# The low parts of the projections' split weights: a negation on ScalarE and an accumulating DMA in place of a subtraction on VectorE

## The chip, the cores and the metric

The kernel runs on one core of one Trainium2 chip. The metric is device time in microseconds (us), lower is better: the median of 3 runs. A profile of one further execution, taken by the hardware profiler, tells what each engine did when.

## The reference, cut to what matters

One layer of a decoder with 1088 token columns (1024 prompt positions and 64 sample tokens) and a width of 1024, all in float32:

```python
p = rmsnorm(x, norm1) @ w_in                  # 1024 -> 1536: 512 for S5, 1024 for the chunked gMLP
o_s5 = S5 scan of p[:, :512], then gelu, then g * sigmoid(g @ w_glu + b_glu)
o_cm = u * (tril(W_s) v + b)                  # 8 heads, chunks of 128 positions
x = x + concat(rmsnorm(o_s5), rmsnorm(o_cm)) @ w_out
x = x + (silu(h @ w_gate) * (h @ w_up)) @ w_down   # h = rmsnorm(x), 22 tiles of 128 hidden columns
y = rmsnorm(x)
```

The projections' weights that the change is about are w_in (12 chunks), w_out (14 chunk loads) and w_glu (2 chunks). A chunk is 128 partitions by 1024 float32 values, 512 KB, and each partition's 4 KB lie together in DRAM.

## The kernel before, in words

TensorE multiplies in a rounded format (float32r). So every operand is split into a high part (the value rounded) and a low part (the value minus its high part), and each product is three matmuls: high by high, high by low, low by high (`mm3`, lines 143 to 146). L144, L145 and L146 in the profile are these three. For `pu`, `po` and `pg` the weight's low part is read by L146; for `pv`, where the weights are the moving operand, by L145.

A split is made by `split` (lines 139 to 141): ScalarE copies the raw chunk into the high tile (L140), VectorE subtracts the high tile from the raw chunk into the low tile (L141). `load_q` (L224) takes a raw buffer (three of 4 KB per partition turn about), has SyncE load the chunk (L227) and splits it. Its high and low tiles are three slots each in one buffer, `cwr` in the profile; later w_out chunks use the same slots (`WO`) and a fourth one in `fb`. A slot is written anew only when TensorE has done its last matmul with the chunk that was there. In a quarter of w_in, chunk 0 holds the first four k-tiles and chunk 1 the last four. For quarters 1 to 5, so, the slot for one chunk of the next quarter comes free shortly before that quarter begins.

The work goes in this order. Quarters 0 and 1 of w_in make the S5 input (`s5_in`), while VectorE computes the S5 tables and the norms of three groups of columns. At the start GpSimd computes `dt` and `mag`, each with a power instruction (L212). Quarters 2 and 3 make v (`v_quarter`), quarters 4 and 5 make u (`cm_out`), with the eight steps of the S5 scan (`s5_a`, `s5_b`, `s5_c`) between them. Then come the GLU with w_glu (`glu`), the output projection (`wo_tile`, `wo_last`) and, from about 428 us to the end, the feed-forward part, a seven-product scheme whose weights are split by a function of its own (`wsplit`), which the change leaves alone.

Each engine takes its instructions from a queue in order. The order on each queue is planned when the kernel is built, from the framework's own estimate of durations (`schedule_with_timeline_sim=True`), with the order of the program text as priority; a few `issue_after` lines pin single places. Here GpSimd issues no DMA before the change: all loads and stores go out on SyncE's queue.

Of the kernel before, what the change touches and what calls it, by code (L numbers as in the profile page):

```python
# [10 lines left out]
F32 = mybir.dt.float32  # L11
F32R = mybir.dt.float32r
I32 = mybir.dt.int32
AF = mybir.ActivationFunctionType
ALU = mybir.AluOpType
# [67 lines left out]
def layer_kernel(ctx: ExitStack, tc: tile.TileContext, A, O, dbg=None):  # L83
    nc = tc.nc
    V, S, P, PE, Q = nc.vector, nc.scalar, nc.gpsimd, nc.tensor, nc.sync
# [46 lines left out]
    def raw(name, shape):  # L132
        n = int(np.prod(shape))
        t = rawp.tile([128, 1024], F32, tag="raw", name=name, bufs=3)[:, :n]
        if len(shape) == 2:
            t = t.rearrange("p (a b) -> p a b", a=shape[0])
        return t

    def split(src, hi, lo, eng=None):
        S.activation(hi, src, AF.Copy)  # L140
        return (eng or V).tensor_tensor(lo, src, hi.bitcast(F32), ALU.subtract)  # L141

    def mm3(p, wh, wl, ah, al, start, stop):
        PE.matmul(p, wh, ah, start=start, stop=False)  # L144
        PE.matmul(p, wh, al, start=False, stop=False)  # L145
        return PE.matmul(p, wl, ah, start=False, stop=stop)  # L146
# [77 lines left out]
    def load_q(key, src, to=None):  # L224

        r = raw(f"w{key[0]}{key[1]}{key[2]}", (4, 256))
        Q.dma_start(r, src)  # L227
        h, l = to or [wqp.tile([128, 4, 256], F32R, tag=x, name=x) for x in ("wqh", "wql")]
        split(r, h, l)
        WQ[key] = (h, l)  # L230

    def load_wq(q):
        for half in range(2):
            load_q(("i", q, half), A["w_in"][q, :, 4 * half:4 * half + 4, :])
# [33 lines left out]
    def fm_group(q, c, tag="mm"):  # L268

        n0, n = CH[c]  # L270
        pp = [bank(f"pu{m}", tag)[:, :n] for m in range(2)]
        km = [(k, m) for k in range(8) for m in range(2)]
        for k, m in km if q == 0 else sorted(km, key=lambda x: x[1]):
            wh, wl = wq(q, k, slice(128 * m, 128 * m + 128))
            MM[q, c] = mm3(pp[m], wh, wl, xh[:, k, n0:n0 + n], xl[:, k, n0:n0 + n], k == 0, k == 7)
        return pp
# [13 lines left out]

    load_x(0, 0)
    load_q(("i", 0, 0), A["w_in"][0, :, 0:4, :])
    load_x(0, 1)
    load_q(("i", 0, 1), A["w_in"][0, :, 4:8, :])
    load_x(0, 2)
    load_x(0, 3)
# [298 lines left out]
    r = raw("bdr", (8, 64))  # L595
# [16 lines left out]
    r = raw("wsr", (8, 128))  # L612
# [4 lines left out]
    for q in range(2):  # L617
# [3 lines left out]
        for i in range(4):  # L621
            m, h = divmod(4 * q + i, 2)
# [6 lines left out]
    def v_quarter(q, j):  # L629
        p = bank("pv")  # L630
        for k in range(8):
            wh, wl = wq(q, k, slice(0, 256))
            mm3(p[:, 0:256], xh[:, k, tok(j)], xl[:, k, tok(j)], wh, wl, k == 0, k == 7)
        S.activation(v[:, j, 256 * (q - 2):256 * (q - 1)], p[:, 0:256], AF.Gelu_apprx_tanh, scale=r1c[:, j:j + 1])
# [98 lines left out]
    wgh = gl.tile([128, 4, W], F32R, name="wgh")  # L733
    wgl = gl.tile([128, 4, W], F32R, name="wgl")
    for i in range(2):
        r = raw(f"wg{i}", (2, W))
        Q.dma_start(r, A["w_glu"][:, 2 * i:2 * i + 2, :])
        split(r, wgh[:, 2 * i:2 * i + 2, :], wgl[:, 2 * i:2 * i + 2, :])
    G5 = []
    for m in range(4):  # L740
        g5 = gl.tile([128, 8, 136], F32, name=f"g5{m}")
# [9 lines left out]
    def glu(c):  # L751
        n0, n = CH[c]
        acc = ACC5[c] = gl.tile([128, 384], F32, tag="acc", name="acc", bufs=3)[:, :n]
        for m in range(4):
            p = bank("pg", "s5" if m % 2 else "mm")
            for k in range(4):
                mm3(p[:, :n], wgh[:, k, 128 * m:128 * m + 128], wgl[:, k, 128 * m:128 * m + 128],
                    xh[:, k, n0:n0 + n], xl[:, k, n0:n0 + n], k == 0, k == 3)
            sg = gl.tile([128, 384], F32, tag="sg", name="sg", bufs=2)[:, :n]
            S.activation(sg, p[:, :n], AF.Sigmoid, bias=gcol("bglu", m))  # L760
            z = tc2n(G5[m], n0, n)
            V.tensor_tensor(z, z, nat(sg), ALU.mult)
            accum_sq(gl, nat(acc), z, m == 0)
# [27 lines left out]
    i = 0  # L791
# [519 lines left out]
```

## Time and profile before

| | |
|---|---|
| median of 3 runs | 1127.18 us (1125.74 to 1130.81) |
| the profiled execution's own time | 1127.69 us |
| its span, first to last instruction | 1125.6 us |
| TensorE's mean granted clock in it | 0.982 |
| TensorE busy | 1056.9 us, 94% |
| VectorE busy | 907.8 us, 81% |
| ScalarE busy | 449.4 us, 40% |
| GpSimd busy | 316.3 us, 28% |

The rows below name engines as PE (TensorE matmul), PEld (TensorE weight load), DVE (VectorE), ACT (ScalarE), POOL (GpSimd) and SP (SyncE). L140 is line 140 of the kernel. A tile pair `cwr<-wi` reads "writes cwr from wi". Busy shares are averages over the span; the stretches of the kernel have different limits.

### The profile page before, as it was taken

To read this page: it belongs to the slowest core of one execution; us is meant where nothing else is said; L and a number is where in the kernel's file an instruction comes from. 1 tells how busy PE (TensorE), PEld (TensorE's weight loads), DVE (VectorE), ACT (ScalarE), POOL (GpSimd) and SP (SyncE) were. 2 spreads that over 40 slices of the span, in tenths; PEclk is the share of its full clock that TensorE was granted. 3 is DMA by queue.
4 is the path that set the end of the run, shared out by engine and by line. 5 is a ranking of instruction groups with operands and counts; after the bars stand their busy time and mean duration, and the time that the engine had idled before them with its cause. 6 is when DMAs were issued, how large, how long until landed. Compare 5 with 4: busy or idle time off the path is not lost.

```text
span 1125.6 us, 20406 instructions
## 1 busy us (share of the span) xinstructions
PE 1056.9 (94%) x7966; PEld 1029.3 (91%) x7966; DVE 907.8 (81%) x1780; ACT 449.4 (40%) x822; POOL 316.3 (28%) x287
## 2 busy tenths in 40 slices
PE   7799999978899989999999999999999999999994
PEld 6789999868799879999999999999998899899994
DVE  6987999889999897667657656657668979879998
ACT  7314334398454442232232232233234324425561
POOL 5010330000000344334334334435434331223220
PEclk9989999989899899999999999999999999999998
DMA  8342334251533113223223223133156815514304
GB/s 272 106 116 74 96 114 153 76 181 43 192 102 101 50 56 127 69 95 127 69 95 126 68 97 125 57 108 126 57 186 213 291 38 184 179 52 135 130 16 158
DMA packets 81519, 131.19 MB, mean 117 GB/s; under 512 B 8976, under 2 KB 60048, under 8 KB 81296
## 3 DMA queue, kind: packets, MB, share of 16 engines
q1 hardware_dynamic: 81424, 129.91, 35.5%
q8 instruction: 62, 1.02, 0.4%
q14 instruction: 33, 0.27, 0.1%
HBM read 90.43 MB, written 34.24 MB: 111 GB/s over the span
## 4 chain that ended last, share of the span: by engine, by line
PE 68%; DVE 19%; DMA 6%; issue 4%; ACT 3%; POOL 1%; SPq 0%; DVEq 0%; ACTq 0%; POOLq 0%
PE u L146 16%; PE u L144 16%; PE u L145 16%; DMA h<-hid_d 4%; DVE xl L141 3%; PE pu L144 2%; PE pu L146 2%; PE pu L145 2%; PE po L146 2%; PE po L144 2%; PE po L145 2%; PE pv L145 2%; PE pv L146 2%; PE pv L144 2%; DVE cwr L141 1%
## 5 line engine op out<-in xcount | busy, mean ns | idle before, releaser
L144 PE MATMUL u<-xh,h 128*128 128x272 f32 x516 | 149.5, 290 | 1.9 <-ACT h L140 1.7
L146 PE MATMUL u<-xh,h 128*128 128x272 f32 x516 | 149.1, 290 | 1.3 <-DVE h L141 1.3
L145 PE MATMUL u<-xl,h 128*128 128x272 f32 x516 | 149.0, 289 | 1.2 <-DVE xl L141 1.2
L144 PE MATMUL u<-xh,fb 128*128 128x272 f32 x382 | 110.5, 289 | 0.6 <-DVE x1r L1108 0.4
L145 PE MATMUL u<-xl,fb 128*128 128x272 f32 x382 | 110.4, 289 | 0.6 <-DVE xl L141 0.6
L146 PE MATMUL u<-xh,fb 128*128 128x272 f32 x382 | 110.3, 289 | 0.2 <-DVE fb L141 0.2
L1023 POOL TENSOR_TENSOR tS<-q,q 128x512 f32<-128x512 f32 x22 | 29.1, 1321 | 262.3 <-DVE h L888 158.4
L144 PEld LDWEIGHTS u<-xh,h 128*128 128x128 f32 x516 | 97.4, 189 | 2.7 <-ACT h L140 2.1
L146 PEld LDWEIGHTS u<-xh,h 128*128 128x128 f32 x516 | 97.4, 189 | 1.9 <-DVE h L141 1.9
L145 PEld LDWEIGHTS u<-xl,h 128*128 128x128 f32 x516 | 97.5, 189 | 1.4 <-DVE xl L141 1.4
L140 ACT ACTIVATE h<-q 128x512 fp32r<-128x512 f32 (+1 forms) x83 | 51.1, 615 | 82.0 <-PE u L145 75.8
L144 PE MATMUL pu<-xh,cwr 128*128 128x384 f32 (+1 forms) x192 | 66.4, 350 | 9.0 <-DVE us L287 9.0
L141 DVE TENSOR_TENSOR h<-q,h 128x512 fp32r<-128x512 f32 (+1 forms) x83 | 68.7, 830 | 6.4 <-ACT h L140 5.3
L145 PEld LDWEIGHTS u<-xl,fb 128*128 128x128 f32 x382 | 72.3, 189 | 1.0 <-DVE xl L141 0.9
L144 PEld LDWEIGHTS u<-xh,fb 128*128 128x128 f32 x382 | 72.2, 189 | 1.0 <-DVE x1r L1108 0.6
L146 PEld LDWEIGHTS u<-xh,fb 128*128 128x128 f32 x382 | 72.0, 189 | 0.4 <-DVE fb L141 0.4
L1061 ACT ACTIVATE st<-st 128x272 f32<-128x272 f32 x88 | 37.8, 431 | 71.2 <-DVE st L1083 35.1
L145 PE MATMUL pu<-xl,cwr 128*128 128x384 f32 (+1 forms) x192 | 65.2, 341 | 0.0
L146 PE MATMUL pu<-xh,cwr 128*128 128x384 f32 (+1 forms) x192 | 65.1, 342 | 0.0
L140 ACT ACTIVATE fb<-q 128x512 fp32r<-128x512 f32 (+1 forms) x64 | 38.7, 607 | 61.2 <-PE u L145 48.3
L1028 POOL TENSOR_TENSOR tS<-tS,q 128x512 f32<-128x512 f32 x22 | 29.8, 1354 | 114.6 <-DVE h L141 61.3
L144 PE MATMUL u<-cwr,h 128*128 128x272 f32 x189 | 55.1, 292 | 1.6 <-ACT cwr L140 1.0
(439 smaller groups left out, 3765.7 us busy)
## 6 DMA issues: line engine op xcount, KB each, us to landing
hid_d<-st SPq DMA_DIRECT2D x22, 952.0 KB, 4.2
h<-hid_d SPq DMA_DIRECT2D x28, 544.0 KB, 3.9
q<-in_w_gate_dram SPq DMA_DIRECT2D x22, 512.0 KB, 3.5
q<-in_w_up_dram SPq DMA_DIRECT2D x22, 512.0 KB, 3.5
q<-in_w_d_dram SPq DMA_DIRECT2D x16, 512.0 KB, 3.9
wo<-in_w_out_dram SPq DMA_DIRECT2D x14, 512.0 KB, 4.2
wi<-in_w_in_dram SPq DMA_DIRECT2D x12, 512.0 KB, 4.9
h<-hid_d SPq DMA_DIRECT2D x14, 408.0 KB, 3.2
```

Source lines behind the costliest of these rows:

```text
L140: S.activation(hi, src, AF.Copy)
L141: return (eng or V).tensor_tensor(lo, src, hi.bitcast(F32), ALU.subtract)
L144: PE.matmul(p, wh, ah, start=start, stop=False)
L145: PE.matmul(p, wh, al, start=False, stop=False)
L146: return PE.matmul(p, wl, ah, start=False, stop=stop)
L1023: P.tensor_tensor(tS, a21, a22, ALU.add)
L1028: P.tensor_tensor(tS, tS, a11, ALU.subtract)
L1061: S.activation(dst, src, AF.Silu)
```

## The change

`load_q` and the two loads of w_glu no longer call `split`, but a new function. ScalarE copies the raw chunk into the high tile as before, then writes the negated high tile into the low tile. GpSimd then issues a DMA that reads the chunk a second time from DRAM and adds it to the low tile. VectorE takes no part, and the raw buffer is read by the first ScalarE instruction alone. All 28 chunks of w_in, w_out and w_glu go this way.

```diff
+    def wsplit_d(raw_, src, hi, lo):
+
+        S.activation(hi, raw_, AF.Copy)
+        S.activation(lo, hi.bitcast(F32), AF.Copy, scale=-1.0)
+        P.dma_start(lo, src, accum_op=ALU.add)
+
...
         Q.dma_start(r, src)
         h, l = to or [wqp.tile([128, 4, 256], F32R, tag=x, name=x) for x in ("wqh", "wql")]
-        split(r, h, l)
+        wsplit_d(r, src, h, l)
         WQ[key] = (h, l)
...
         Q.dma_start(r, A["w_glu"][:, 2 * i:2 * i + 2, :])
-        split(r, wgh[:, 2 * i:2 * i + 2, :], wgl[:, 2 * i:2 * i + 2, :])
+        wsplit_d(r, A["w_glu"][:, 2 * i:2 * i + 2, :], wgh[:, 2 * i:2 * i + 2, :], wgl[:, 2 * i:2 * i + 2, :])
```

## Rows read from the trace of the kernel before

**Rows 1.** The page's part 1: busy us (share) xinstructions.

```profile
PE 1056.9 (94%) x7966; PEld 1029.3 (91%) x7966; DVE 907.8 (81%) x1780; ACT 449.4 (40%) x822; POOL 316.3 (28%) x287
```

**Rows 2.** Busy time by stretch: length, engines (xinstructions), granted clock, DMA share, GB/s.

```profile
0.00:84.00 84.00, 68.63 (x373) 63.80 (x374) 72.27 (x226) 32.88 (x63) 19.64 (x32) 0.94 0.52 164
84.00:224.00 140.00, 138.80 (x1071) 129.90 (x1070) 129.09 (x288) 54.09 (x123) 24.29 (x29) 1.00 0.36 102
224.00:280.00 56.00, 44.84 (x276) 41.66 (x276) 51.42 (x97) 49.74 (x77) 0.00 (x0) 0.94 0.37 115
280.00:308.00 28.00, 22.60 (x165) 21.99 (x164) 26.33 (x46) 11.95 (x16) 0.00 (x0) 0.88 0.54 181
```

**Rows 3.** The chain of waits in order of time: start, us, what.

```profile
38.46 1.14 DVE cwr L141
...
221.93 1.15 DVE cwr L141
...
232.87 0.98 DVE wgl L141
...
305.27 1.14 DVE fb L141
```

**Rows 4.** Instructions on raw chunks of w_in: ns min/median/max, first and last start.

```profile
L140 ACT ACTIVATE cwr<-wi x12: 1042/1057/1065, 7.2 to 176.5; 128x1024 fp32r<-128x1024 f32 x12
L141 DVE TENSOR_TENSOR cwr<-wi,cwr x12: 1182/1224/1271, 8.2 to 180.8; 128x1024 fp32r<-128x1024 f32 x12
...
DMA to landing us min/median/max: 3.6/4.9/9.7
```

**Rows 5.** DMA issues: KB each, median us from issue to landing.

```profile
x1a<-in_xT_dram SPq DMA_DIRECT2D x1, 1088.0 KB, 6.4
```

**Rows 6.** Timeline of GpSimd: start, us, engine, line, what [idle before <-releaser].

```profile
2.55 5.46 POOL L212 TENSOR_TENSOR dt<-eb,s5i 128x32 f32<-128x32 f32 x1
...
9.99 5.63 POOL L212 TENSOR_TENSOR mag<-eb,ld 128x32 f32<-128x32 f32 x1
...
16.10 0.25 POOL L214 TENSOR_TENSOR mag<-mag,magt 128x32 f32<-128x32 f32 x1
...
140.26 2.72 POOL L641 TENSOR_TENSOR mv<-mv,mhalf 128x1 f32<-128x1 f32 x1 [0.33 <-DVE mv L640]
...
153.86 0.65 POOL L641 TENSOR_TENSOR mv<-mv,mhalf 128x1 f32<-128x1 f32 x1 [0.76 <-DVE mv L640]
```

**Rows 7.** Timeline of TensorE's matmuls, same columns.

```profile
10.56 0.81 PE L146 MATMUL pu<-xh,cwr 128*128 128x384 f32 x2
...
56.76 0.66 PE L144 MATMUL pu<-xh,cwr 128*128 128x384 f32 x1 [6.99 <-DVE us L287]
...
77.16 0.28 PE L146 MATMUL pv<-cwr,xl 128*128 128x256 f32 x1
...
109.08 0.40 PE L144 MATMUL pv<-cwr,xh 128*128 128x256 f32 x2
...
144.94 0.33 PE L145 MATMUL pu<-xl,cwr 128*128 128x384 f32 x1
```

**Rows 8.** Timeline of ScalarE, same columns.

```profile
7.18 1.04 ACT L140 ACTIVATE cwr<-wi 128x1024 fp32r<-128x1024 f32 x1
...
22.45 0.56 ACT L165 ACTIVATE rsy<-ss,epsc 128x384 f32<-128x384 f32 x1
...
71.93 1.06 ACT L140 ACTIVATE cwr<-wi 128x1024 fp32r<-128x1024 f32 x1 [6.59 <-PE pu L145]
...
104.31 1.06 ACT L140 ACTIVATE cwr<-wi 128x1024 fp32r<-128x1024 f32 x1 [0.53 <-PE pv L146]
...
140.99 1.06 ACT L140 ACTIVATE cwr<-wi 128x1024 fp32r<-128x1024 f32 x1
...
227.16 1.06 ACT L140 ACTIVATE cwr<-wo 128x1024 fp32r<-128x1024 f32 x1 [0.88 <-DMA wo<-in_w_out_dram]
```

**Rows 9.** Timeline of VectorE, same columns.

```profile
24.30 0.55 DVE L166 SCALAR_TENSOR_TENSOR rsa<-ss,rsy 128x384 f32<-128x384 f32 x1
```

## The prediction

> **What bounds the kernel now.** I read the page first, then the busy times by stretch, then the chain of waits, and last the timelines of the places where a weight chunk is split and first used. Over the whole span TensorE is busy 94% [rows 1], but the share hides stages with different limits. By stretches [rows 2], VectorE leads from 0 to 84 us (72.3 of 84 us, TensorE 68.6 with 373 matmuls), TensorE from 84 to 224 (138.8 of 140), VectorE and ScalarE together from 224 to 280 (51.4 and 49.7 of 56), and VectorE alone from 280 to 308 (26.3 of 28). Behind that TensorE is the limit again, and no weight of the feed-forward part is touched. So the change can only win or lose in the first 308 us, and what it does there moves everything behind it as a block.
>
> The chain of waits says where a subtraction of a weight chunk sets the end. Of the 28, ten lie on it, each with 0.98 to 1.15 us, the first at 38.46 and the last at 305.27 [rows 3]: two before 84 us, four between 221.93 and 249, four between 279 and 305.27. I count 1.1 us each. The other 18 are work that VectorE does while something else is awaited, and their removal frees it for nothing.
>
> **What the change takes away.** VectorE loses 28 subtractions of 1.22 us [rows 4], 34 us in all, but on the chain only 10 x 1.1 = 11 us: 2.2 before 84 us, 4.4 from 221 to 249, 4.4 from 279 to 306. The raw buffer comes free when ScalarE has read it, no longer when VectorE has. That matters once: at 227.16 ScalarE stood 0.88 us for a w_out chunk whose load had waited for a raw buffer [rows 8]. I count 0.9 us won there.
>
> **What it adds on ScalarE.** 28 negations. Their form (128x1024, rounded format out) is that of the copy before them, so 1.06 us each [rows 4]; below by nothing, above by the 1.06 to 1.07 of the slowest copy, since only the scale differs. In most stretches they lie beside ScalarE's idle time (54.1 of 140 us busy, 12.0 of 28 [rows 2]) and cost nothing. From 224 to 280 there is no such cover: four chunks fall there, 4.2 us more on an engine with 6.3 us free in 56, in a part of the chain that changes between ScalarE and VectorE. I count all 4.2. If ScalarE's free time covers them it is 0. In the first 20 us three negations stand between the splits of x; they are covered by the wait described next, and cost up to 3.2 us if that wait is gone.
>
> **What it adds as a wait.** The low part was there 1.22 us after VectorE took it up. Now it is there when a DMA that GpSimd issues after the negation has landed. The trace shows no DMA issued by GpSimd and none that adds. Bounds: 3.6 us, the quickest plain load of the same 512 KB, and 9.7 us, the slowest [rows 4]. The adding DMA has to read its destination too, twice the bytes in, and the row nearest to that is the load of 1088 KB with 6.4 us [rows 5]. I take 6.4 us from the end of the negation, or from the time GpSimd is free, to the landing; GpSimd's own time for issuing is in it.
>
> By the Trainium skill (DMA: Bandwidth & Descriptors, section on the anatomy of a DMA on the gpsimd path) such a DMA takes 2.0 us plus its bytes over 436 GB/s, which would be an estimated 3.2 us for 512 KB. That is a little under the quickest load of the same size in this trace; the rule says nothing of adding, and by it the sum below would come out near +1 us instead of +9.
>
> Where is a low part needed sooner than that?
>
> Start. GpSimd's queue has the two powers: the first from 2.55, the second from 9.99 to 15.62, and the chain that ends with `mag` is done at 16.10 + 0.25 = 16.35 [rows 6]. These are written ahead of the first chunk and depend on one early load only, so I expect the DMA of chunk 0 behind them on the queue, although its negation is done by 7.18 + 1.04 + 1.06 = 9.3 [rows 8]. It lands at 16.35 + 6.4 = 22.75. TensorE stands at its first low-part matmul at 10.56 [rows 7], so it waits 12.2 us, and behind it in the same queue wait the sums of squares of the first column group. For those waits ScalarE's reciprocal root, which ended at 22.45 + 0.56 = 23.0 [rows 8], and for that VectorE's L166 at 24.30 [rows 9], with 1.3 us to spare. VectorE leads this stretch, so 12.2 - 1.3 = 10.9 us come through, less the 2.2 us of the two chain subtractions: **+8.7**. From below: issued between the two powers (at 9.9) and landed in 3.6, the wait is 2.9 us and the sum is -0.6. From above, with 9.7: +12.
>
> Changes of quarter. Three chunks are split only when TensorE frees their slot, shortly before their first use. The copy starts at 71.93, 104.31 and 140.99 [rows 8]; copy, negation and DMA (1.06 + 1.06 + 6.4) end at 80.5, 112.8 and 149.5. TensorE reached the low part at 77.2, 109.1 and 144.9 [rows 7]. That is 3.3 + 3.7 + 4.6 = 11.6 us of standing, in a stretch that TensorE bounds. The S5 scan's matmuls are independent and can be planned into these gaps, so the cost lies between 0 and 11.6; I take about half, **+6**. The other chunks are split well ahead of their use; for them the DMA is hidden behind the matmuls of the quarter before, and without that cover each would cost what these three do. In the GLU the low part comes later too, but TensorE's results there wait for ScalarE's long run of splits anyhow, so I count nothing.
>
> 224 to 280: -4.4 - 0.9 + 4.2 = **-1.1**. 280 to 308: **-4.4**; the w_out chunks are ready long before use there.
>
> Sum: 8.7 + 6 - 1.1 - 4.4 = +9.2 us on the profiled execution's own 1127.69, which is 0.5 above the median of the runs: 1127.2 + 9.2 = **1136.4 us**.
>
> **Rivals.** (a) The relief wins. GpSimd's DMA for chunk 0 goes out between the two powers and low parts land as fast as the fastest plain load. Then the start is -0.6, the quarter changes are nearly free, and the sum is -0.6 - 1.1 - 4.4 = -6, about 1121 us. It decides from a landing of 3.6 us and an issue before 10 us on. For it speaks that the negation is done at 9.3, just ahead of the second power at 9.99 [rows 6]; against it, that the power is earlier in the text and ready at the same time. (b) It comes out even. TensorE has 6.99 us of idle time before 56.76 [rows 7], waiting for VectorE. If VectorE's small table work is planned into the wait, most of the late start is caught up there: 9.2 - 7 = +2, about 1129 us. Against it, VectorE's queue is in order and L166 stands early in it. (c) The issue itself is slow. On GpSimd the same small power took 0.65 us at one time and 2.72 at another [rows 6], beside a busy VectorE. If issuing suffers likewise and a landing takes 12 us, the start is +14.3, the quarter changes 28.4 us of standing, half of it counted 14, and the sum is +23, about 1150 us. The Trainium skill (SBUF — State Buffer, section on who interferes with whom) says that VectorE instructions in a two-port mode shut GpSimd out while it writes descriptors for a DMA; by that rule (c) is what happens wherever VectorE's copies and tensor-scalar operations are dense. No run here shows a DMA issued by GpSimd.
>
> **How the numbers follow.** My forecast has 0.43 (its own range 1132 to 1144), (a) 0.14, (b) 0.25, (c) 0.18. Differences within 0.5%, 5.6 us, are about what a measurement can't tell from no change: that is 1121.5 to 1132.8. (a) is faster, (b) is the same, the forecast and (c) are slower: 0.14, 0.25, 0.61. The range leaves out about half of (a) and half of (c): 1121 to 1152 us.
>
> **What the changed profile would show.** If I am right, GpSimd's first DMA stands behind `mag`, near 16.4 us; TensorE has a gap of some 10 us before its first L146, and L166 moves from 24.3 to about 35; PE waits of 2 to 4 us stand at two or three changes of quarter; the ten subtractions are gone from the chain, with negations and DMAs into `cwr` on it instead; from 280 to 308 the stretch gets 4 us shorter; from the feed-forward part on both traces run alike. Wrong would make it a first DMA issued near 10 us, landings far from 6.4 us, or a plan that orders the other queues quite differently.

## The result and the profile after

The changed kernel takes 1157.62 us, median of 4 runs (1154.37 to 1160.24), beside 1128.41 us for the kernel before on the same chip. The ratio is 1.0256, 95% interval 1.0228 to 1.0284: 29 us slower, outside my range of 1121 to 1152. Below, the microseconds beside a ratio are the ratio less one, times the median of before in that comparison (1128 to 1130 us).

The page of the changed kernel, parts 1 and 3 (part 3: queue, packets, MB, share of 16 DMA engines):

```profile
PE 1075.4 (93%) x7966; PEld 1041.0 (90%) x7966; DVE 877.2 (76%) x1752; ACT 475.0 (41%) x850; POOL 332.6 (29%) x315
...
q1 hardware_dynamic: 81424, 129.91, 34.4%
q0 software_dynamic: 4032, 14.68, 7.4%
```

Beside [rows 1], VectorE has 28 instructions and 31 us less, ScalarE 28 instructions and 26 us more, so the change does what it says. A second queue is there now, with 14.68 MB. In the changed kernel L145, L146 and L147 are the copy, the negation and the accumulating DMA, and L150, L151 and L152 the three matmuls that were L144 to L146; each edit below moves the lines a little further. The busy time by stretch, to be held against [rows 2], and then the kernel before from 308 to 364 us, which [rows 2] leaves out:

```profile
0.00:84.00 84.00, 68.84 (x344) 61.23 (x344) 63.58 (x217) 39.72 (x72) 25.91 (x39) 0.92 0.65 181
84.00:224.00 140.00, 128.76 (x962) 119.72 (x960) 111.90 (x260) 55.06 (x119) 23.77 (x33) 0.98 0.55 136
224.00:280.00 56.00, 48.68 (x285) 44.41 (x286) 40.52 (x79) 40.16 (x62) 4.54 (x7) 0.88 0.65 174
280.00:308.00 28.00, 23.32 (x164) 21.46 (x162) 25.02 (x50) 23.46 (x36) 0.86 (x1) 1.00 0.53 152
308.00:364.00 56.00, 49.82 (x367) 48.40 (x368) 43.72 (x90) 30.36 (x45) 4.85 (x6) 0.97 0.54 133
```

```profile
308.00:364.00 56.00, 54.63 (x432) 54.26 (x431) 52.57 (x94) 27.68 (x45) 0.00 (x0) 1.00 0.33 109
```

Count TensorE's matmuls: by 84 us 344 instead of 373, from 84 to 224 us 962 instead of 1071. It is 138 matmuls behind at 224 us, some 18 us at 138.80 us / 1071 each. Between 224 and 308 us it makes up 8 of them. From 308 to 364 us, where by my prediction nothing could be won or lost any more, it falls behind by another 65: 195 in all, some 25 us at the same price. VectorE's load fell in every stretch, and its idle time bought nothing. The DMA share rose in all of them but 280 to 308, and most, from 0.37 to 0.65, between 224 and 280 us, where TensorE lost no matmuls: the share alone doesn't tell where the loss is.

The same 7966 matmuls are busy for 18.5 us longer (1075.4 against 1056.9), while TensorE's idle time in the span (1156.6 against 1125.6 us) grew by 12.5 only. Part of that is TensorE's clock: its mean granted clock was 0.972 in this execution and 0.982 in that of the kernel before, which by itself makes an estimated 11 of the 18.5 us (1056.9 x 0.982 / 0.972). It is a rough share, for over all executions the two kernels had 0.971 to 0.975 and 0.972 to 0.985. No list of waits shows it.

What TensorE waited for (line, tile, releaser: us in total, times, longest), the rows that end in a DMA:

```profile
PE yb L575 <- DMA mb<-mb: 4.0, 1, 4.0
PE pg L152 <- DMA wgl<-in_w_glu_dram: 3.9, 1, 3.9
PE po L152 <- DMA fb<-in_w_out_dram: 3.6, 1, 3.6
...
PE pv L151 <- DMA cwr<-in_w_in_dram: 3.1, 1, 3.1
PE sb L499 <- DMA U<-us_d: 3.1, 2, 1.7
PE pu L152 <- DMA cwr<-in_w_in_dram: 2.8, 2, 1.8
PE po L152 <- DMA cwr<-in_w_out_dram: 2.6, 1, 2.6
```

Low parts account for 16.0 us of waiting (3.9 + 3.6 + 3.1 + 2.8 + 2.6). Another 7.1 us went to transfers that the change doesn't touch, the scan's `mb` and `U`; in the kernel before, the only such row is 1.2 us for `mb`. The accumulating DMAs by their line (ns of the issue; then landing), in place of [rows 4, 5]:

```profile
L147 POOL DMA_DIRECT2D cwr<-in_w_in_dram x12: 862/866/1061, 14.8 to 197.9; - x12
...
DMA to landing us min/median/max: 5.7/7.5/12.5
```

And GpSimd's first one, in place of [rows 6]:

```profile
9.01 5.44 POOL L218 TENSOR_TENSOR mag<-eb,ld 128x32 f32<-128x32 f32 x1
14.43 0.46 POOL L219 TENSOR_SCALAR magt<-ld 128x32 f32<-128x32 f32 x1
14.83 1.06 POOL L147 DMA_DIRECT2D cwr<-in_w_in_dram  x1
```

It stands behind the second power, as forecast, at 14.83 us; TensorE's wait for it ends at 22.58 us (22.75 forecast for the landing). That agreement is luck: the issue came 1.5 us earlier than I had it, and the landing took 7.7 us and not 6.4. And TensorE has only 1.82 us of idle time right before it:

```profile
22.58 0.69 PE L152 MATMUL pu<-xh,cwr 128*128 128x384 f32 x1 [1.82 <-DMA cwr<-in_w_in_dram]
```

The planner put the sums of squares of the first column group in front of it, which I had behind it in the queue. The stretch isn't cheap for that: TensorE has done 29 matmuls by 24 us, 80 in the kernel before. But the instruction of [rows 9], which hangs on those sums and which I expected to move from 24.30 to about 35 us, starts earlier:

```profile
22.78 0.55 DVE L172 SCALAR_TENSOR_TENSOR rsa<-ss,rsy 128x384 f32<-128x384 f32 x1
```

Every queue has another order than before, which is why parts had to be tried one by one, and then in a held order.

### The profile page after: what moved, and what is told of

Read it like the earlier page. It is cut to its first block, busy times and chain, and to the rows that moved or that the text cites. A ratio compares the mean times of both kernels' runs of the same rounds, so it can differ in the third digit from the quotient of the medians.

```text
span 1156.6 us, 20454 instructions
## 1 busy us (share of the span) xinstructions
PE 1075.4 (93%) x7966; PEld 1041.0 (90%) x7966; DVE 877.2 (76%) x1752; ACT 475.0 (41%) x850; POOL 332.6 (29%) x315
## 3 DMA queue, kind: packets, MB, share of 16 engines
q1 hardware_dynamic: 81424, 129.91, 34.4%
q0 software_dynamic: 4032, 14.68, 7.4%
## 4 chain that ended last, share of the span: by engine, by line
PE 56%; issue 12%; DMA 12%; DVE 12%; ACT 5%; POOL 2%; SPq 0%; DVEq 0%; POOLq 0%; ACTq 0%
PE u L152 15%; PE u L150 14%; PE u L151 14%; DMA h<-hid_d 4%; DVE xl L141 2%; PE pu L152 2%; PE pu L150 2%; PE pu L151 2%; DMA cwr<-in_w_in_dram 2%; PE pv L152 1%; PE pv L151 1%; PE pv L150 1%; ACT xh L140 1%; DMA bdr<-in_bd_dram 1%; DMA hid_d<-st 1%
## 5 line engine op out<-in xcount | busy, mean ns | idle before, releaser
L150 PE MATMUL u<-xh,h 128*128 128x272 f32 x516 | 149.3, 290 | 2.0 <-ACT h L140 1.8
L152 PE MATMUL u<-xh,h 128*128 128x272 f32 x516 | 149.1, 289 | 1.8 <-DVE h L141 1.8
L151 PE MATMUL u<-xl,h 128*128 128x272 f32 x516 | 149.0, 289 | 0.7 <-DVE xl L141 0.7
L150 PE MATMUL u<-xh,fb 128*128 128x272 f32 x382 | 110.5, 289 | 0.6 <-DVE x1r L1114 0.4
L151 PE MATMUL u<-xl,fb 128*128 128x272 f32 x382 | 110.3, 289 | 0.6 <-DVE xl L141 0.6
L152 PE MATMUL u<-xh,fb 128*128 128x272 f32 x382 | 110.3, 289 | 0.5 <-DVE fb L141 0.5
L150 PEld LDWEIGHTS u<-xh,h 128*128 128x128 f32 x516 | 97.4, 189 | 2.7 <-ACT h L140 2.2
L152 PEld LDWEIGHTS u<-xh,h 128*128 128x128 f32 x516 | 97.4, 189 | 2.2 <-DVE h L141 2.2
L151 PEld LDWEIGHTS u<-xl,h 128*128 128x128 f32 x516 | 97.5, 189 | 1.0 <-DVE xl L141 0.9
L150 PEld LDWEIGHTS u<-xh,fb 128*128 128x128 f32 x382 | 72.2, 189 | 1.0 <-DVE x1r L1114 0.6
L151 PEld LDWEIGHTS u<-xl,fb 128*128 128x128 f32 x382 | 72.2, 189 | 1.0 <-DVE xl L141 0.9
L152 PEld LDWEIGHTS u<-xh,fb 128*128 128x128 f32 x382 | 71.9, 188 | 0.8 <-DVE fb L141 0.8
L1067 ACT ACTIVATE st<-st 128x272 f32<-128x272 f32 x88 | 37.9, 431 | 73.0 <-DVE st L1089 35.9
L152 PE MATMUL pu<-xh,cwr 128*128 128x384 f32 (+1 forms) x192 | 64.6, 342 | 2.8 <-DMA cwr<-in_w_in_dram 2.8
L150 PE MATMUL pu<-xh,cwr 128*128 128x384 f32 (+1 forms) x192 | 66.5, 347 | 0.0
L151 PE MATMUL pu<-xl,cwr 128*128 128x384 f32 (+1 forms) x192 | 65.9, 344 | 0.0
L150 PE MATMUL po<-xh,cwr 128*128 128x272 f32 x192 | 57.9, 302 | 5.9 <-ACT sg L766 3.5
```

Of the source, the lines that this page charges most:

```text
L1067: S.activation(dst, src, AF.Silu)
```

## Experiments

Four theories: **L**, the wait for each landing; **T**, the traffic of the DMAs delays other transfers; **N**, the negations on ScalarE; **P**, the new order of the queues.

**The change by kind of weight.** The other chunks are split by VectorE as before.

```diff
-        wsplit_d(r, src, h, l)
+        (wsplit_d(r, src, h, l) if key[0] == "i" else split(r, h, l))
```

> Only the 12 chunks of w_in get the negation and the accumulating DMA; w_out and w_glu are split as before. Theory L (the landing of each low part: TensorE stands where a chunk is used soon after its slot came free) puts here what the stretches up to the end of the projections lost, 3.7 us at the start and 18.7 us to the end of the last w_in group: +22 us, about 1150. Theory T (the DMAs themselves: 14.7 MB more traffic that delays other loads, wherever they stand) goes by bytes: 12 of 28 DMAs, 12/28 of 29 = +12 us, about 1140.

> Only the 14 chunks of w_out get the negation and the accumulating DMA; w_in and w_glu are split as before. Theory L: the 7.7 us that the stretch of the output projection lost, +8 us, about 1136. Theory T, by bytes: 14 of 28 DMAs, +14.5 us, about 1143. My prediction had -4 to -5 us for them (they are ready long before use): about 1123.

w_in alone: ratio 1.0110 (1.0077 to 1.0144), +12.4 us. w_out alone (`"o"`): 1.0098 (1.0083 to 1.0113), +11.1 us. Together 23.5 of the 29; w_glu was not run alone. The w_out chunks, for which I had forecast a gain, cost nearly as much as w_in. The number for w_in is T's (+12, against +22 for L); that for w_out lies between the two (+8 for L, +14.5 for T) and decides nothing.

**The change without its DMA.** First VectorE adds the raw chunk to the negation, then nothing does: the second run leaves the adding out, and its low parts are minus the high part.

```diff
         S.activation(lo, hi.bitcast(F32), AF.Copy, scale=-1.0)
-        P.dma_start(lo, src, accum_op=ALU.add)
+        V.tensor_tensor(lo, lo.bitcast(F32), raw_, ALU.add)
```

> ScalarE makes the copy and the negation as in the changed kernel, but VectorE adds the raw chunk to it; no DMA is issued by GpSimd. Theories L and T both put the loss on the DMA: here 0 to +4 us, 1128 to 1132 (the low part comes 1.1 us later, and nothing is taken from VectorE). Theory N (28 more instructions on ScalarE are the cost, in its busy stretches from 224 to 308 us and in front of the splits of x): +10 us or more, 1138 and up.

> ScalarE makes the copy and the negation, and nothing adds the raw chunk: the low parts are left wrong (minus the high part). This is the change without its DMA, so it shows what the relief of VectorE is worth with no landing to pay. Theories L and T: -6 to -11 us, 1117 to 1122, since ten subtractions of 1.1 us lay on the chain, less up to 4.2 for ScalarE. Theory N: 0 or slower, 1128 and up.

VectorE adds: 1.0079 (1.0048 to 1.0110), +8.9 us. Nobody adds: 0.9956 (0.9941 to 0.9971), -5.0 us. So the relief is there, near my -7, and the DMA costs some 34 us on top of it, the change of order that comes with it included. The +8.9 fits none of L and T, and is close to N's bound.

**Is it the negation, or any edit?** A one-column negation behind each of the 28 copies; then whole negations into a scratch, for seven chunks.

```diff
+        S.activation(warm, hi[:, 0, 0:1].bitcast(F32), AF.Copy, scale=-1.0)
         V.tensor_tensor(lo, raw_, hi.bitcast(F32), ALU.subtract)
```

```diff
         V.tensor_tensor(lo, raw_, hi.bitcast(F32), ALU.subtract)
+        scr = s5p.tile([128, 4, 256], F32R, tag="scr", name="scr")
+        S.activation(scr, hi.bitcast(F32), AF.Copy, scale=-1.0)
```

> The kernel before, with one more instruction on ScalarE behind each of the 28 copies: a negation of a single column into a tile that nobody reads (some 0.2 us each, an estimate from ScalarE's shortest rows, under 6 us in all and not waited for by anything). VectorE subtracts as before, no DMA. Theory P (the planner lays every queue anew from its own costs whatever is edited, and the order it had for the kernel before was a good draw): +3 to +9 us from this alone. Theory N (the negations' 28 us of ScalarE are what cost 9 us in the run where VectorE adds): 0 to +1.5.

> For the seven slack chunks of w_in ScalarE also makes a negation, into a scratch that nobody reads; VectorE subtracts as before and no DMA is added. It is the partner of the next run. Theory N: 7 of 28 negations, +2. Theory P: anything from 0 to +9. If both are wrong: 0 to +0.5.

Tiny ones: 1.0022 (1.0011 to 1.0033), +2.5 us. Seven whole ones: 0.9999 (0.9988 to 1.0011), nothing. N falls for those seven. What the 28 with VectorE adding pay for stays open between ScalarE's crowded stretch behind 224 us and the order.

**My own terms, one by one.** Only the named w_in chunks get the change.

```diff
-        wsplit_d(r, src, h, l)
+        (wsplit_d(r, src, h, l) if key in (("i", 2, 1), ("i", 3, 1), ("i", 4, 1)) else split(r, h, l))
```

> Only the two chunks of the first quarter of w_in get the negation and the accumulating DMA. My prediction's first term by itself: +8.7 us, 1138. By the changed kernel's profile, where the first quarter pair ended 3.7 us late (6.4 with w_in alone): +4 to +6, 1132 to 1135. If the loss sits in traffic or in re-ordering later on: 0 to +1.

> Only the three chunks (2,1), (3,1) and (4,1) of w_in, whose slot comes free shortly before their use, get the negation and the accumulating DMA. My prediction's second term by itself: +6 us, between 0 and +11.6, so about 1135. Theory L: the whole of what the two stages behind the start lost, +10 or more. Theory T (traffic): 3 of 28 DMAs, +3.

> Only the seven w_in chunks that I had called well ahead of their use get the negation and the accumulating DMA: (1,0), (1,1), (2,0), (3,0), (4,0), (5,0) and (5,1). My prediction: 0 (hidden behind the matmuls of the quarter before), 1127 to 1131. Theory T: 7 of 28 DMAs, +7, with loads that they delay as the waits.

Start: 1.0026 (1.0012 to 1.0040), +2.9 us, where I had 8.7. Quarter changes: 0.9988 (0.9975 to 1.0001), -1.4 us, no loss that can be told, where I had 6. The seven that I had called hidden: 1.0091 (1.0065 to 1.0117), +10.3 us. They sum to 11.8, near the 12.4 of w_in as a whole, but the loss sits on the other side of my list. In the run of the seven TensorE waits little for low parts:

```profile
PE pg L150 <- ACT xh L140: 6.9, 1, 6.9
...
PE sb L499 <- DMA U<-us_d: 3.9, 1, 3.9
...
PE yb L575 <- DMA mb<-mb: 1.8, 1, 1.8
...
PE pu L152 <- DMA cwr<-in_w_in_dram: 1.0, 1, 1.0
```

1.0 us for its own DMAs, 5.7 us for the scan's, and 6.9 us (3.0 in the kernel before) for ScalarE's split of what the scan brings. This last row is no mark of the seven: it is 10.1 us in the start run. So the next run takes TensorE's wait for the low parts away and leaves the traffic.

**The DMA with no reader.** VectorE subtracts as before; for the seven chunks the negation and the accumulating DMA go into a scratch.

```diff
         S.activation(scr, hi.bitcast(F32), AF.Copy, scale=-1.0)
+        P.dma_start(scr, src, accum_op=ALU.add)
```

> As the run before, and GpSimd's accumulating DMA of each of the seven slack chunks goes into that scratch: traffic, issue and ScalarE's work as in the run with the seven slack chunks (+9.9 us), but no instruction of the kernel waits for the landing. Theory T (other loads are delayed by the traffic): +7 to +10, with loads of U or the scan's tables slower. Theory L (the wait for the landing): 0 to +2, as in its partner. Theory P: a number that fits neither, with another order.

1.0052 (1.0033 to 1.0071), +5.9 us, against nothing without the DMA. More than half of the +10.3 needs no matmul that waits for a landing. One thing still waits: the seven share one scratch, and ScalarE stood 2.5 us once until an earlier DMA had landed there.

**A plain DMA, and GpSimd as the subtracter.**

```diff
-        S.activation(lo, hi.bitcast(F32), AF.Copy, scale=-1.0)
-        P.dma_start(lo, src, accum_op=ALU.add)
+        P.dma_start(lo, src)
```

```diff
-        S.activation(lo, hi.bitcast(F32), AF.Copy, scale=-1.0)
-        P.dma_start(lo, src, accum_op=ALU.add)
+        P.tensor_tensor(lo, raw_, hi.bitcast(F32), ALU.subtract)
```

> GpSimd's DMA stays, but as a plain load that writes the raw chunk into the low part: no negation, no adding (the low parts are left wrong). If adding is what makes a landing slow (theory A), it lands like the plain loads of the same size on SyncE's queue, 4 to 5 us median, and the time falls to 1135 to 1142. If it is the path that GpSimd issues, or the other loads in flight (theory Q), landings stay at 6 to 8 us and the time at 1145 to 1155, less only what the negations cost.

> The 28 subtractions move to GpSimd: no negation, no DMA. VectorE is relieved as in the change. An instruction of this size takes GpSimd some 2 to 3 us by its other tensor operations here (an estimate), so the low part comes 1 to 2 us later than before instead of 6 or more. Theory L: the relief stays and the delay is small, 1118 to 1128, the version that beats both. Theory P: within +-6 of before. If GpSimd and VectorE slow each other: +5 or more.

Plain: 1.0072 (1.0049 to 1.0095), +8.1 us. The landing of 5.8 us in the median lies between what the two theories of that run expected (4 to 5 and 6 to 8), the time in the range of the first, A. It also has no negation to wait for, so its time is no price of the adding alone. Its line:

```profile
L146 POOL DMA_DIRECT2D cwr<-in_w_in_dram x12: 527/542/697, 1.3 to 189.5; - x12
...
DMA to landing us min/median/max: 3.9/5.8/11.0
```

Beside it the accumulating DMA's median landing is 7.5 us instead of 5.8 and its issue 0.87 us instead of 0.54, though at other moments and beside other transfers. Nearer to a price of the adding is what the same 14.68 MB on the same queue took of the DMA engines, 4.4% of the span here and 7.4% in the changed kernel:

```profile
q0 software_dynamic: 4032, 14.68, 4.4%
```

GpSimd's subtraction: 1.0186 (1.0168 to 1.0203), +21.0 us. By form, on GpSimd (busy us, mean ns):

```profile
L146 POOL TENSOR_TENSOR cwr<-wo,cwr 128x1024 fp32r<-128x1024 f32 x11 | 37.3, 3390 | 99.6 <-ACT cwr L145 99.6
...
L146 POOL TENSOR_TENSOR cwr<-wi,cwr 128x1024 fp32r<-128x1024 f32 x12 | 32.5, 2716 | 60.7 <-ACT cwr L145 34.9 <-issue 25.8
```

One takes 2.7 to 3.4 us in the mean, but 2.4 to 2.6 in the median of these two groups, within my estimate of 2 to 3; a single one of 8.65 us lifts the mean. Yet the run that I expected to beat both kernels loses 21 us. How that divides between the later low part and the order was not followed up.

**Work or order?** Every run so far also had an order of its own. So each instruction that two kernels share was chained to the one before it, as it stands in the order wanted (issue order only, no wait for its end), on all five queues; `NEW` holds those that only one kernel has.

```diff
+    for e, z in HELD.items():
+        at = [i for i in nc.cur_bb.bb.instructions if str(i.engine).endswith("." + e)
+              and not type(i).__name__.startswith("Bass") and i.name not in NEW]
+        order = array.array("H", zlib.decompress(base64.b85decode(z)))
...
+        for a, b in zip(order, order[1:]):
+            tc.add_manual_dep(at[b], at[a].name, mybir.DependencyInfo(mybir.DependencyClass.NoSync,
+                              mybir.DependencyReason.DATA), reason="held")
```

> The changed kernel, with every instruction that both kernels have held in the order of the kernel before, on all five queues; only the negations and GpSimd's DMAs are placed freely. Theory P (the new order is the loss): +10 us or less, 1130 to 1138. Theory W (the work itself is: the wait for each low part, traffic, ScalarE): +25 or more, since nothing can be moved into a gap; by my prediction's terms with the quarter changes in full, +15.

> The work of the kernel before (VectorE subtracts, no negation, no DMA), held in the order of the changed kernel; only the 28 subtractions are placed freely. Theory P: +15 us or more, 1143 and up. Theory W: -2 to +5.

| | order of before | order of the changed kernel |
|---|---|---|
| work of before | 1 | 1.0102 (1.0076 to 1.0128), +11.5 us |
| changed work | 1.0377 (1.0346 to 1.0408), +42.6 us | 1.0256, +29 us |

P falls as the whole cause: with the work of before, the order of the changed kernel costs 11.5 us. The changed work costs 42.6 us when nothing may move; the planner gives 14 of it back with that order. The 1 in the table is the kernel before as it is; it was not run with the chain added, but the negation-only run below, chained too, is faster than it, so the chain itself can't be what costs the 42.6. In the old order TensorE's waits for low parts are:

```profile
PE pu L156 <- DMA cwr<-in_w_in_dram: 16.0, 4, 11.7
PE po L156 <- DMA cwr<-in_w_out_dram: 7.3, 2, 5.6
...
PE pg L156 <- DMA wgl<-in_w_glu_dram: 6.8, 1, 6.8
...
PE pv L155 <- DMA cwr<-in_w_in_dram: 6.3, 2, 3.2
...
PE po L156 <- DMA fb<-in_w_out_dram: 1.5, 1, 1.5
```

37.9 us, against 16.0 in the order of its own. The first is 11.7 us long, and the two `pv` rows are the changes of quarter, up to 3.2 each.

**Parts in the old order.** The negation without the DMA (nothing adds); the traffic of the seven chunks with no reader; w_out alone; the start alone. The edits are those above, in the held order.

> ScalarE's negation in place of VectorE's subtraction and no DMA (nothing adds the raw chunk, so the low parts are left wrong), in the order of the kernel before. This prices the relief of VectorE with ScalarE's work and no re-ordering: by my prediction -11 + 4.2 = -7; in an order of its own it was -5.

> VectorE subtracts as before, and for the seven slack chunks of w_in ScalarE's negation and GpSimd's accumulating DMA go into a scratch that nobody reads, in the order of the kernel before. Theory T (traffic delays other loads): +4 to +6, as in the run with an order of its own (+5.9). Theory P: 0 to +1, that run's loss was its order.

> Only the 14 w_out chunks get the negation and the accumulating DMA, in the order of the kernel before. My prediction (ready long before use): -4 to -5 us. By the waits for w_out low parts that the changed work shows in the old order (1.5, 1.7 and 5.6 us, with half clock behind them): +7 to +11, like the +11 in an order of its own.

> Only the two chunks of the first quarter get the negation and the accumulating DMA, in the order of the kernel before. My prediction's first term: +8.7 to +10.9. By the lag of TensorE that the changed work shows behind the first wait in the old order: +13 to +15, of which an order of its own gives back all but 3.

Negation alone: 0.9975 (0.9959 to 0.9992), -2.8 us. That is what the change could win at best in this order. Beside the +42.6 it prices the 28 DMAs, with everything that waits for them, at some 45 us. Traffic: 1.0084 (1.0063 to 1.0104), +9.5 us, so T stands with the order fixed. That is more than the +4 to +6 that I expected of T; this run has the seven negations too, which had no partner run in the held order; in an order of their own they cost nothing. ScalarE waits once for the scratch, 1.4 us. w_out: 1.0123 (1.0082 to 1.0164), +13.9, more than the +7 to +11 expected. Start: 1.0123 (1.0089 to 1.0157), +13.9.

How traffic becomes time can be followed in the traffic run. Timelines of GpSimd and SyncE, VectorE and TensorE:

```profile
110.33 0.85 POOL L154 DMA_DIRECT2D scr<-in_w_in_dram  x1 [3.56 <-ACT scr L153]
110.50 0.62 SPq L511 DMA_DIRECT2D Sw<-Ss  x1
...
118.45 0.69 DVE L550 TENSOR_TENSOR Ss<-Ss,CO 128x512 f32<-128x512 f32 x1 [3.92 <-DMA Sw<-Ss]
...
120.49 0.30 PE L499 MATMUL ptr<-idn,PT 128*128 128x128 f32 x1 [2.56 <-DVE PT L490]
```

The scan's swap `Sw<-Ss` (128 KB) is issued 0.17 us behind the accumulating DMA, whose issue to landing is 7.9 us. The issues of that moment, there and (second fence) in the kernel before from 100 to 112 us (KB, median us to landing):

```profile
scr<-in_w_in_dram POOLq DMA_DIRECT2D x1, 512.0 KB, 7.9
Sw<-Ss SPq DMA_DIRECT2D x2, 128.0 KB, 5.1
```

```profile
Sw<-Ss SPq DMA_DIRECT2D x2, 128.0 KB, 2.4
```

The pair's median of 5.1 is that of one as before and one that landed only with the big DMA. VectorE stood 3.92 us for it, and TensorE 2.56 us for VectorE, in a stretch that TensorE bounds. It isn't the only such place: before 250 us VectorE waits 16.6 us in this run for the scan's swaps and loads (`Sw`, `gw` and `bc`), 6.2 us in the kernel before and 7.5 in the run with the seven negations and no DMA, where VectorE has the same work. By the Trainium skill (DMA: Bandwidth & Descriptors, section on queues, rings and completion order) each DMA engine serves the queues that have work for it by turns, a packet at a time; that a small copy beside a large one lands with it agrees with that, for the large one has fewer packets (4032 for 28 DMAs, so 144 of some 3.6 KB each) than the small one, which the kernel cuts into rows of 512 bytes (an estimated 256). The turns themselves stand in no view here.

The w_out run shows the same on the way to a late landing. ScalarE, TensorE, then the issues from 340 to 350 us:

```profile
352.40 0.63 ACT L144 ACTIVATE fb<-q 128x512 fp32r<-128x512 f32 x1 [7.32 <-DMA q<-in_w_gate_dram]
...
355.59 1.04 ACT L149 ACTIVATE cwr<-wo 128x1024 fp32r<-128x1024 f32 x1
...
366.33 0.60 PE L159 MATMUL po<-xh,cwr 128*128 128x272 f32 x1 [5.93 <-DMA cwr<-in_w_out_dram]
```

```profile
cwr<-in_w_out_dram POOLq DMA_DIRECT2D x1, 512.0 KB, 9.1
q<-in_w_gate_dram SPq DMA_DIRECT2D x1, 512.0 KB, 8.5
```

A feed-forward weight lands in 8.5 us instead of 4.3, ScalarE stands in its queue for it (7.32 us, 4.93 in the kernel before), the copy of the w_out chunk behind it is late (355.59), then come the negation and the landing. In the kernel before that copy and the first use of the low part are:

```profile
348.97 1.06 ACT L140 ACTIVATE cwr<-wo 128x1024 fp32r<-128x1024 f32 x1
...
356.70 0.29 PE L146 MATMUL po<-xh,cwr 128*128 128x272 f32 x1
```

From start of the copy to use are 7.7 us: room for a subtraction, none for a negation and a landing (1.06 + 1.06 + 6.4 us by my own terms). The row that I should have looked for; it lies behind 308 us.

The start run has the mechanism of my first term, undiluted. TensorE in the start run, then its busy time by stretch, then the same stretch of the kernel before:

```profile
23.52 0.69 PE L159 MATMUL pu<-xh,cwr 128*128 128x384 f32 x1 [11.32 <-DMA cwr<-in_w_in_dram]
...
70.67 0.66 PE L157 MATMUL pu<-xh,cwr 128*128 128x384 f32 x1 [5.31 <-DVE us L300]
```

```profile
24.00:29.00 5.00, 5.00 (x17) 4.70 (x16) 0.00 (x0) 0.00 (x0) 0.00 (x0) 0.50 0.68 182
```

```profile
24.00:29.00 5.00, 5.00 (x30) 5.00 (x30) 4.94 (x11) 2.83 (x7) 0.00 (x0) 1.00 0.40 87
```

11.32 us of standing (12.2 forecast from 10.56 [rows 7]). Behind it the granted clock is 0.50, 1.2 GHz, and TensorE does 17 matmuls where it did 30: about 2 us that I had not counted. Shorter waits for a low part are followed by the lower level as well: in the 2 us behind 100.40 us of the changed work in the old order (a wait of 3.10 us ends at 98.41), behind 260.80 us of the changed kernel (3.94 us, to 258.85) and behind 368.30 us of the w_out run in the old order (5.93 us, to 366.33) the granted clock is 0.50. Of the 6.99 us before 56.76 [rows 7], 5.31 are left at 70.67, so 1.7 us come back (1.3 counted as slack). The matmul of 10.56 came 13.0 us late (23.52), that of 56.76 13.9 us late, as much as the run lost.

## Why the prediction was wrong

The sign was right, for half of the reason. What failed is the part on **what the change adds as a wait**, in its answer to where a low part is needed sooner: everything outside the start and the three changes of quarter was put at nothing, or at a gain.

1. *"The other chunks are split well ahead of their use; for them the DMA is hidden."* This step failed. The seven cost +10.3 us. I had looked for who waits for the new DMA, and not for who shares the DMA engines with it. The same seven DMAs with no reader cost +5.9 in an order of their own and +9.5 in the old one, through late transfers of the scan. And two of the seven are not quite hidden: in the old order, with all 28 changed, TensorE waits 2.1 us at 58.62 us and 1.9 at 215.52, in quarters 1 and 5.
2. *"The w_out chunks are ready long before use"*, counted as -4.4 from 280 to 308, is the same step, and by size the larger miss: +11.1 alone, +13.9 in the old order. I had looked "there" alone, from 280 to 308, and with *"the change can only win or lose in the first 308 us"* no further: the last two w_out chunks are copied at 348.97 and 350.94 us, the tightest place leaves 7.7 us from copy to use, and the changed kernel falls 65 matmuls further behind between 308 and 364 us.
3. *"In the GLU ... I count nothing"*: TensorE waits 3.9 us there, 6.8 in the old order.
4. The start, +8.7: the mechanism is right (11.32 or 11.67 us of waiting, 12.2 forecast), the size is not. In the old order it is +13.9, by the half clock that follows, and because the 2.2 us that I set against it belong to subtractions of other chunks (38.46 us [rows 3] and after). In an order of its own it is +2.9, and there it is rival (b) that came true: TensorE still falls far behind, 73 matmuls by 40 us instead of 181, with a wait of 8.22 us for ScalarE's splits of x, and catches most of it up from 40 to 84 us (44.00 us busy with 274 matmuls, 35.04 with 198 in the kernel before), where its 9.0 us of waiting for VectorE's `us` are gone. Whether VectorE's table work moved as (b) had it was not followed.
5. The quarter changes, +6: in the old order 3.1 and 3.2 us of waiting at two of the three (3.3, 3.7 and 4.6 forecast); with an order of their own, -1.4, nothing, and TensorE's list of waits names no low part. That other matmuls can be planned into these gaps was right, and more so than the half that I took; which ones they were was not looked up.
6. Relief of VectorE less the negations, -11 + 4.2: -5.0 in an order of its own, -2.8 in the old one. Sign right, size somewhat too large.
7. The landing of 6.4 us: 7.5 in the median, six of 28 beyond my upper bound of 9.7, to 12.5. Each of these six had another accumulating DMA issued within 3.3 us of it. Too short, yet not what failed. By the Trainium skill (DMA: Bandwidth & Descriptors, section on the anatomy of a DMA on the gpsimd path) it would be an estimated 3.2 us; the quickest accumulating one took 5.7 and a plain one 3.9, and the measurement decides.

That w_in as a whole came out near my terms for it, 12.4 us against 8.7 + 6 = 14.7, is luck: the start and the quarter changes cost 13 us less than I had, and the seven that I had at nothing 10 us more.

Of the rivals, (c) came nearest to the time, 1150 us, but the slow issue that it rests on was not there: GpSimd's issues took 0.85 to 1.06 us everywhere, beside a busy VectorE too. Landings of 11.7 and 12.5 us, as (c) had them, came for the two w_glu chunks alone. By the rule that I had cited for it (the Trainium skill, SBUF — State Buffer, section on who interferes with whom) they could have been held up; no row here shows an issue that was. Nor is GpSimd's own queue, which now waits for ScalarE's negations, what holds the others up: in the changed kernel no wait for GpSimd's work before 430 us is longer than 2.8 us.

In the changed kernel, 16.0 us of waits for low parts and the 11.5 us of the order make 27.5 of the 29. That sum is only an account: the order run has neither the traffic nor the relief, the lower clock behind the waits isn't in it, and how these divide the rest was not measured. Open are also the +8.9 us of the run where VectorE adds, and w_glu by itself.

No version here that still makes the low parts beats the kernel before: the three quarter chunks alone come out even, and all the relief without any DMA, so without the low parts, is worth 2.8 to 5.0 us.

## What to carry to other kernels

When a step moves from an engine to a DMA, price it three times: the landing at the tightest place of each chunk (from when its slot is free to its first use, from rows, also for the chunks that look early), what else is in flight beside it and who waits for that, and the clock that TensorE loses behind a new wait of some microseconds. Look to the last use of the last chunk, not to the stretch where the step seems to matter. With a planner, try the edit also in the held order of the kernel before: it shows the work's price at its place, while an order of its own spreads it over rows that look unrelated. And ask first what the relief could be worth at best: the run that leaves the step out altogether gained 5 us.

## What the runs showed of the hardware that I had not expected

- An accumulating DMA of 512 KB from GpSimd: 0.85 to 1.06 us of GpSimd for the issue (0.54 in the median for a plain one), 5.7 / 7.5 / 12.5 us to the landing (min, median, max; plain 3.9 / 5.8 / 11.0).
- Its queue held 7.4% of the DMA engines for 14.68 MB, the other queue 34.4% for 129.91 MB: 0.50 against 0.26% per MB, 1.9 times. Plain DMAs of the same 14.68 MB from GpSimd held them for 4.4%, so the accumulating ones took 1.7 times as long.
- A 128 KB copy issued 0.17 us behind such a DMA landed with it, after 7.9 us (the longest such copy in the kernel before took 5.2); the pair's median went from 2.4 to 5.1 us. A 512 KB load beside two of them went from 4.3 to 8.5.
- Waits of 3.1, 3.9, 5.9 and 11.3 us for a low part were each followed by a granted clock of 0.50 on TensorE.
- A GpSimd subtraction of 128x1024 took 2.4 to 2.6 us in the median, VectorE's 1.22 [rows 4].
